# First norm taken tile by tile, weight splits of the first products put behind the rows, and transposes of the identity without a reader on TensorE

## The chip, the core and the metric

The program runs on one core of one Trainium2 chip. Its engines work side by side, each through a list of instructions of its own: TensorE (PE; its weight loads are shown as PEld), VectorE (DVE), ScalarE (ACT) and GpSimd (POOL). SyncE (SP) issues nearly all the transfers. The metric is the time of one execution on the device in microseconds (us); the median of three runs is compared.

## The reference

One layer over 512 rows of 1024 float32 numbers, and 256 memory rows. What bears on the change is its beginning:

```python
h = rmsnorm(x, g_mix_pre[l])          # x * rsqrt(mean(x*x) + EPS) * g
proj = h @ w_in[l]
aq, ak, av, iq, ik, iw, bq, bk, bv, cq, gate_logits = jnp.split(proj, split_points, axis=-1)
...
mkv = rmsnorm(mem, g_mem[l]) @ w_mem_kv[l]
...
x = x + rmsnorm(merged @ w_out[l], g_mix_post[l])
h = rmsnorm(x, g_ffn_pre[l])
gu = h @ w_ffn_in[l]
f = (jax.nn.silu(gu[..., :D_FF]) * gu[..., D_FF:]) @ w_ffn_out[l]
x = x + rmsnorm(f, g_ffn_post[l])
```

Between the projections and `merged` stand three kinds of attention: sparse attention over keys that an index (iq, ik, iw) selects, stick-breaking attention, and attention into the memory rows (with the queries cq).

## The kernel before

Every matrix product is made from split operands: a float32 number is taken as a high part of reduced precision and a low part (the rest), and a product is the sum of three passes, high by high, high by low and low by high (`passes`, L85 to L87). Making the two parts is called a split: ScalarE casts the high part (L74, or L78 with a gain), VectorE or GpSimd subtracts it from the source for the low part (L75, L79).

The stage of the change is `first` (L362 to L440). The rows x come in four tiles of 128 rows. For each tile `squares` sums the squares of its two halves (L231 on ScalarE, L229 on VectorE), `rstd1` adds them up on VectorE (L240) and raises them to the power -1/2 on GpSimd (L241), `rstd2` refines that with two small VectorE operations (L246, L247), and `scaled` multiplies the tile (L251; tiles 0 and 1 on VectorE, 2 and 3 on GpSimd). Then PE transposes each tile in eight pieces of 128 x 128 (L385). A bank of PSUM takes the piece k of two tiles, a pair, and the split of that bank with the gain of the norm (L78, L79) gives 256 columns of the transposed activations `hT[k]`. Products with two weight tiles follow, for each pair 24 passes per weight: the index keys (`w_ik`, 72 columns wide) and the first tile of cq (`w_cq`, 128 wide). The eight banks of PSUM are shared, so the transposes of the last pieces of tiles 2 and 3 wait for banks that a split of the same pair frees.

After this stage PE transposes a table (L331), makes another (L341), and goes on with four index-query tiles (`feat_tiles` with the columns from C_IQ), of which each needs a load of 512 KB by SyncE (L95, three buffers `wraw`), a cast (L74) and a low part (L75). The memory rows are loaded and normed beside these.

What sets the order: PE's list is in the order in which the code is written, in the whole program. In `first` VectorE, ScalarE and GpSimd are in written order too. Outside it a scheduler of the framework orders them; so in the kernel before, the splits of the first two index-query tiles stand on VectorE and ScalarE between the splits of pair 0 and those of pair 1. Each engine works its list strictly in order, as does SyncE with its transfers.

Of the kernel before, what the change touches and what calls it, by code (L numbers as in the profile page):

```python
# [17 lines left out]
P = 128  # L18
T = 512
D = 1024  # L20
NK = D // P
# [11 lines left out]
C_AQ, C_AK, C_AV, C_IQ, C_IK, C_BQ, C_BK, C_BV, C_CQ, C_G = (  # L33
    0, 512, 1024, 1536, 2048, 2120, 2632, 3144, 3656, 4168)
# [13 lines left out]
class Layer:  # L48
# [32 lines left out]
    def passes(self, out, pairs, first, last, **kw):  # L81

        n = len(pairs)
        for i, (sh, sl, mh, ml) in enumerate(pairs):
            self.nc.tensor.matmul(out, lhsT=sh, rhs=mh, start=first and i == 0, stop=False, **kw)  # L85
            self.nc.tensor.matmul(out, lhsT=sh, rhs=ml, start=False, stop=False, **kw)  # L86
            self.nc.tensor.matmul(out, lhsT=sl, rhs=mh, start=False, stop=last and i == n - 1, **kw)  # L87
# [90 lines left out]
        self.nc.tensor.matmul(out, lhsT=x, rhs=y[:, 0:n], start=True, stop=False)  # L178
        self.nc.tensor.matmul(out, lhsT=x, rhs=y[:, T:T + n], start=False, stop=True)  # L179

    def feat_tiles(self, w_src, acts, out, js, n=T, t0=0, evac=None):

        per = T // n
        for j in js:
            w = self.weights(w_src[:, j * P:(j + 1) * P], NK, P)
            ps = self.bank()
            yield from self.feat(ps[:, 0:n], w, acts, n=n, t0=t0)
            if evac is not None:
                out[j] = evac(ps)
                continue  # L190
            if j % per == 0:
                slot = self.big("act")
            o = (j % per) * 2 * n
            out[j] = slot[:, o:o + n], slot[:, o + n:o + 2 * n]
            self.split(*out[j], ps[:, 0:n])
# [65 lines left out]
    def run(self):  # L261
        w_in, w_kv = self.a["w_in"], self.a["w_mem_kv"]
        late = ExitStack()
        att = ExitStack()
        self.att = att.enter_context(self.tc.tile_pool(name="att", bufs=1))
        with self.tc.manual_schedule(engines={mybir.EngineType.PE}):
            self.setup()
            memT, mk, mv, cq = [], {}, {}, {}
            self.index_keys(cq)
            xs = [self.load_rows(self.a["mem"], t) for t in range(2)]  # L270
            for x in xs:
                self.norm_in(x)

            self.iq = {}
            iqs = lambda js: self.feat_tiles(w_in[:, C_IQ:C_IQ + 512], self.hT, self.iq, js, T - P, P,
                                             lambda ps: self.evac_q(ps[:, 0:T - P], T - P))
            cqs = lambda js: self.feat_tiles(w_in[:, C_CQ:C_CQ + 512], self.hT, cq, js)
            mks = lambda js: self.feat_tiles(w_kv[:, 0:512], memT, mk, js, n=M)
            mvs = self.tok_tiles(w_kv[:, 512:1024], memT, (0, 1), mv)
            memTs = self.mem_T(xs, memT)  # L280
            iq = self.add(iqs(range(4)))
            kv = self.add(cqs((1,)), self.mix(memTs, cqs((2,)), 2), mks(range(4)), cqs((3,)), mvs)
            self.drain(iq)
            self.scores()
            self.drain(kv)
            a, aq = self.qkv(C_AQ, C_AK, C_AV)
            self.branch_c(cq, mk, mv)
            self.acc = {}
            self.add(self.merge(2, self.outC, "w_up_c"))
            self.drain(aq)  # L290
            self.select()
            self.fill(FM)
            b, bq = self.qkv(C_BQ, C_BK, C_BV)
            self.branch_a(*a)
            self.drain(bq)
            self.add(self.merge(0, self.outA, "w_up_a"))
            self.outB = []
            self.add(self.merge(1, self.outB, "w_up_b"))
            self.branch_b(*b)
            self.drain()  # L300
            att.close()
            self.late = late.enter_context(self.tc.tile_pool(name="late", bufs=1))
            self.mix_out()
            self.ffn()
        late.close()
# [56 lines left out]
    def first(self, x, row, w_ik, w_cq):  # L362

        nc = self.nc
        self.hT = [self.pair("h") for _ in range(NK)]
        self.first_ps = self.bank(), self.bank()
        half = [slice(0, 256), slice(256, 512)]
        ms, bank = {}, {}

        def squares(t):  # L370
            ms[t] = self.squares([x[t][:, 0:512], x[t][:, 512:1024]], both=True)

        def mean(t):
            ms[t] = self.rstd1(ms[t])

        def scale(t):
            self.scaled(x[t], x[t], self.rstd2(ms[t]), nc.gpsimd if t > 1 else None)

        def trans(t, ks=range(NK)):
            for k in ks:  # L380
                b = t // 2, k
                if b not in bank:
                    bank[b] = self.bank()
                c = (t % 2) * P
                nc.tensor.transpose(bank[b][:, c:c + P], x[t][:, k * P:(k + 1) * P], self.ident)  # L385

        def split(pr, k):
            hi, lo = self.hT[k]
            self.split_gain(hi[:, half[pr]], lo[:, half[pr]], bank[pr, k][:, 0:256], self.cols[:, k:k + 1])

        def product(pr, i, k, w):
            c = (72, P)[i]
            self.feat_k(self.first_ps[i][0:c, half[pr]], w, self.hT, k, n=256, t0=256 * pr, c=c)

        squares(0)
        mean(0)
        ps = self.bank()
        nc.tensor.transpose(ps[:, 0:8], row, self.ident[0:8, 0:8])
        nc.vector.tensor_copy(self.cols[:, 0:8], ps[:, 0:8])
        squares(1)  # L400
        mean(1)
        scale(0)
        trans(0, range(5))
        scale(1)
        trans(1, range(5))
        trans(0, range(5, NK))
        trans(1, range(5, NK))
        ik = self.parts(w_ik, ("act", "act"), nc.gpsimd)
        squares(2)
        mean(2)  # L410
        split(0, 0)
        squares(3)
        split(0, 1)
        mean(3)
        scale(2)
        split(0, 2)
        split(0, 3)
        scale(3)
        split(0, 4)
        split(0, 5)  # L420
        cq = self.parts(w_cq, ("act", "act"), nc.gpsimd)
        split(0, 6)
        split(0, 7)
        for k in range(NK):
            product(0, 0, k, ik)
            if k > 3:
                trans(2, (k - 4,))
        for k in range(4):
            trans(3, (k,))
            split(1, k)  # L430
        for k in range(4, NK):
            trans(2, (k,))
            trans(3, (k,))
            split(1, k)
            product(0, 1, k - 4, cq)
        for k in range(4, NK):
            product(0, 1, k, cq)
        for i, w in enumerate((ik, cq)):
            for k in range(NK):
                product(1, i, k, w)  # L440
# [120 lines left out]
    def heads(self, prob, v, out, gap, first):  # L561


        p, pT = {}, {}
        for s in range(9):
            if s < 8:
                p[s] = []
            if s:
                pT[s - 1] = []
            for i in range(NT):  # L570
                if s < 8:
                    p[s].append(prob(s, i))
                if s and i < 3:
                    self.values_T(p[s - 1], i, pT[s - 1])
                if s and i == 3:
                    self.values(pT[s - 1], v, s - 1, out)
                self.fill(gap)
            if s == 0:
                self.fill(first)
# [341 lines left out]
    def ffn(self):  # L921
# [17 lines left out]
        for j, w in enumerate(self.first_ffn):  # L939
            u = (self.bank(), self.bank()), w  # L940
            run(products(*u, 0))
            first.append(u)
# [9 lines left out]
        for j, u in enumerate(first[1:], 1):  # L952
            run(products(*u, 1))
            self.gated(u[0], out(j))
# [9 lines left out]
        class Parts:  # L964
            def __getitem__(_, k):
# [3 lines left out]
                return pairs[k]  # L969

        run(self.tok_pair(w_out, Parts(), NF, range(NT), tail=4))


# [16 lines left out]
```

## Time and profile before

| | us |
|---|---|
| median of 3 runs | 917.26 (917.25 to 917.41) |
| the profiled execution | 917.32 |
| its span, first to last instruction | 915.5 |
| PE busy in the span | 887.9 (97%) |
| VectorE busy | 644.4 (70%) |
| ScalarE busy | 457.6 (50%) |
| GpSimd busy | 122.3 (13%) |

Times in the rows count from the start of the span. A row of a timeline names its start, its length, the engine, the line, the operation, what is written and read, and in brackets how long the engine had been idle before it and what ended that. Rows of one kind that follow each other are taken together (x4), and their length is then that of the whole group. PE's instructions overlap: the distance of two starts says more than the length of one.

### The profile page before, as it was taken

What the parts mean: (1) busy time and instruction counts of PE and PEld (TensorE: products, weight loads), DVE (VectorE), ACT (ScalarE), POOL (GpSimd) and SP (SyncE); (2) the same over time, 40 slices, a digit from 0 to 9 for tenths busy, and PEclk for the clock granted to TensorE, in tenths of its full rate; (3) what the DMA queues carried; (4) which work ended last, traced back from release to release, by engine and by line L of the source; (5) the groups of instructions that cost most, each with busy time, mean ns of one, the idle gap of its engine ahead of it and who ended that gap; (6) DMA issues with size and microseconds to landing.
All of it is one profiled execution on the core that took longest, in us unless ns stands there. A gap on an engine that the chain in (4) does not pass through costs nothing.

```text
span 915.5 us, 13446 instructions
## 1 busy us (share of the span) xinstructions
PE 887.9 (97%) x5110; PEld 780.3 (85%) x5110; DVE 644.4 (70%) x1122; ACT 457.6 (50%) x804; POOL 122.3 (13%) x155
## 2 busy tenths in 40 slices
PE   5999999999999999999999999899999999999997
PEld 4889788888888888888788788899999999888885
DVE  7579999963588976777563478688888887932215
ACT  6365575332576666665353355355555555821111
POOL 4000000020032304443212123400000000000000
PEclk9999999999999999999999999899999999999999
DMA  6433543444354433222473524203334334533102
GB/s 213 127 93 116 175 125 93 127 119 112 103 150 127 127 82 92 69 59 58 136 252 107 184 83 125 69 28 112 107 102 116 97 112 131 168 93 100 38 0 92
DMA packets 129541, 101.17 MB, mean 111 GB/s; under 512 B 4652, under 2 KB 115292, under 8 KB 129476
## 3 DMA queue, kind: packets, MB, share of 16 engines
q1 hardware_dynamic: 128884, 99.26, 37.2%
q10 hardware_dynamic: 592, 1.05, 0.3%
q8 instruction: 40, 0.66, 0.3%
q14 instruction: 25, 0.20, 0.1%
HBM read 93.73 MB, written 2.12 MB: 105 GB/s over the span
## 4 chain that ended last, share of the span: by engine, by line
PE 82%; DVE 9%; issue 3%; ACT 2%; DMA 1%; POOL 1%; POOLq 0%; DVEq 0%; SPq 0%; ACTq 0%
PE bank L85 19%; PE bank L86 19%; PE bank L87 19%; PE bank L734 15%; DVE wl L75 3%; PE bank L534 2%; PE bank L549 1%; PE bank L179 1%; PE bank L178 1%; PE bank L209 1%; PE bank L211 1%; PE bank L210 1%; DMA lraw<-in_w_ffn_in_dram 1%; DVE e L621 1%; DVE score L506 1%
## 5 line engine op out<-in xcount | busy, mean ns | idle before, releaser
L75 DVE TENSOR_TENSOR wl<-wraw,wh 128x1024 fp32r<-128x1024 f32 (+1 forms) x112 | 130.6, 1167 | 100.4 <-ACT wh L74 100.1
L74 ACT CAST wh<-wraw 128x1024 fp32r<-128x1024 f32 (+1 forms) x112 | 107.3, 959 | 141.7 <-PE bank L86 79.5
L85 PE MATMUL bank<-h,wh 128*128 128x512 f32 (+1 forms) x376 | 148.8, 396 | 0.0
L87 PE MATMUL bank<-h,wl 128*128 128x512 f32 (+1 forms) x376 | 145.3, 386 | 1.0 <-DVE wl L75 0.9
L86 PE MATMUL bank<-h,wh 128*128 128x512 f32 (+1 forms) x376 | 145.0, 386 | 0.0
L734 PE MATMUL bank<-w,act 128*128 128x512 f32 x360 | 89.0, 393 | 0.0
L87 PEld LDWEIGHTS bank<-h,wl 128*128 128x128 f32 x376 | 70.6, 188 | 15.9 <-DVE wl L75 1.7
L85 PEld LDWEIGHTS bank<-h,wh 128*128 128x128 f32 x376 | 70.9, 189 | 11.7 <-PE bank L341 0.2
L86 PEld LDWEIGHTS bank<-h,wh 128*128 128x128 f32 x376 | 70.8, 188 | 11.4
L734 PEld LDWEIGHTS bank<-w,act 128*128 128x128 f32 x360 | 67.4, 188 | 15.0
L734 PE MATMUL bank<-wh,act 128*128 128x512 f32 x240 | 72.5, 393 | 0.0
L85 PE MATMUL bank<-act,wh 128*128 128x256 f32 (+1 forms) x204 | 69.2, 339 | 0.7 <-DVE s L896 0.7
L86 PE MATMUL bank<-act,wh 128*128 128x256 f32 (+1 forms) x204 | 67.9, 333 | 0.0
L87 PE MATMUL bank<-act,w 128*128 128x256 f32 x228 | 64.1, 281 | 0.0
L85 PE MATMUL bank<-h,w 128*128 128x256 f32 x228 | 64.1, 281 | 0.0
L86 PE MATMUL bank<-h,w 128*128 128x256 f32 x228 | 64.1, 281 | 0.0
L87 PE MATMUL bank<-h,w 128*128 128x256 f32 x228 | 64.1, 281 | 0.0
L85 PE MATMUL bank<-act,w 128*128 128x256 f32 x228 | 64.1, 281 | 0.0
L86 PE MATMUL bank<-act,w 128*128 128x256 f32 x228 | 64.1, 281 | 0.0
L241 POOL TENSOR_TENSOR rs<-ms,mhalf 128x1 f32<-128x1 f32 x18 | 12.1, 674 | 387.7 <-DVE ms L240 384.0
L598 POOL TENSOR_TENSOR p<-toep,score 128x128 f32<-128x128 f32 (+3 forms) x32 | 31.6, 1001 | 199.2 <-DVE score L507 103.0
L734 PEld LDWEIGHTS bank<-wh,act 128*128 128x128 f32 x240 | 45.0, 188 | 9.9
(189 smaller groups left out, 2113.3 us busy)
## 6 DMA issues: line engine op xcount, KB each, us to landing
wraw<-in_w_in_dram SPq DMA_DIRECT2D x64, 512.0 KB, 3.6
lraw<-in_w_ffn_in_dram SPq DMA_DIRECT2D x22, 512.0 KB, 3.9
wraw<-in_w_ffn_in_dram SPq DMA_DIRECT2D x22, 512.0 KB, 3.7
wraw<-in_w_ffn_out_dram SPq DMA_DIRECT2D x11, 512.0 KB, 3.6
lraw<-in_w_ffn_out_dram SPq DMA_DIRECT2D x11, 512.0 KB, 3.5
wraw<-in_w_mem_kv_dram SPq DMA_DIRECT2D x8, 512.0 KB, 3.7
lraw<-in_w_out_dram SPq DMA_DIRECT2D x6, 512.0 KB, 5.5
wraw<-in_w_out_dram SPq DMA_DIRECT2D x6, 512.0 KB, 3.7
```

Of the source, the lines that this page charges most:

```text
L74: self.nc.scalar.copy(hi, src)
L75: (eng or self.nc.vector).tensor_tensor(lo, src, hi.bitcast(F32), op=OP.subtract)
L85: self.nc.tensor.matmul(out, lhsT=sh, rhs=mh, start=first and i == 0, stop=False, **kw)
L86: self.nc.tensor.matmul(out, lhsT=sh, rhs=ml, start=False, stop=False, **kw)
L87: self.nc.tensor.matmul(out, lhsT=sl, rhs=mh, start=False, stop=last and i == n - 1, **kw)
L178: self.nc.tensor.matmul(out, lhsT=x, rhs=y[:, 0:n], start=True, stop=False)
L179: self.nc.tensor.matmul(out, lhsT=x, rhs=y[:, T:T + n], start=False, stop=True)
L209: self.nc.tensor.matmul(ps, lhsT=ah[:, s], rhs=wh[:, k2], start=st, stop=False)
L241: self.nc.gpsimd.tensor_tensor(r, ms, self.mhalf, op=OP.pow)
L534: self.nc.tensor.transpose(ps[:, c:c + P], p[i][:, j * P:(j + 1) * P], self.ident)
L598: nc.gpsimd.tensor_tensor(s, toep[0][:, 0:n][:, ::-1], self.mask[i], op=OP.add)
L734: self.nc.tensor.matmul(ps[c], lhsT=st_[:, s], rhs=mv_[:, 0, c * 512:(c + 1) * 512], start=f and k == order[0], stop=l and k == order[-1])
```

## The change

`squares` in `first` now takes for each tile whether VectorE shares in it: tiles 0 and 3 are halved between ScalarE and VectorE as before, tiles 1 and 2 are squared by ScalarE alone. Tile 0 is scaled and its first four pieces are transposed before tile 1 is summed on VectorE. The pieces are transposed 4 and 4, before 5 and 3. The low parts of `w_ik` and `w_cq` are made by VectorE, before by GpSimd; that of `w_cq` and its cast stand behind all eight splits of pair 0. The first two index-query tiles are loaded in `first`, and split behind the splits of pair 1; `feat_tiles` takes these two from a list. `warm(n)` writes n transposes of the identity into a bank that nothing reads: 5 and 21 around the transpose of the gain, and 10 between the first pieces of tile 0 and those of tile 1.

```diff
--- before.py
+++ after.py
@@ -178,11 +178,11 @@
         self.nc.tensor.matmul(out, lhsT=x, rhs=y[:, 0:n], start=True, stop=False)
         self.nc.tensor.matmul(out, lhsT=x, rhs=y[:, T:T + n], start=False, stop=True)
 
-    def feat_tiles(self, w_src, acts, out, js, n=T, t0=0, evac=None):
+    def feat_tiles(self, w_src, acts, out, js, n=T, t0=0, evac=None, ws=()):
 
         per = T // n
         for j in js:
-            w = self.weights(w_src[:, j * P:(j + 1) * P], NK, P)
+            w = ws[j] if j < len(ws) else self.weights(w_src[:, j * P:(j + 1) * P], NK, P)
             ps = self.bank()
             yield from self.feat(ps[:, 0:n], w, acts, n=n, t0=t0)
             if evac is not None:
@@ -273,7 +273,7 @@
 
             self.iq = {}
             iqs = lambda js: self.feat_tiles(w_in[:, C_IQ:C_IQ + 512], self.hT, self.iq, js, T - P, P,
-                                             lambda ps: self.evac_q(ps[:, 0:T - P], T - P))
+                                             lambda ps: self.evac_q(ps[:, 0:T - P], T - P), self.w_iq)
             cqs = lambda js: self.feat_tiles(w_in[:, C_CQ:C_CQ + 512], self.hT, cq, js)
             mks = lambda js: self.feat_tiles(w_kv[:, 0:512], memT, mk, js, n=M)
             mvs = self.tok_tiles(w_kv[:, 512:1024], memT, (0, 1), mv)
@@ -367,8 +367,8 @@
         half = [slice(0, 256), slice(256, 512)]
         ms, bank = {}, {}
 
-        def squares(t):
-            ms[t] = self.squares([x[t][:, 0:512], x[t][:, 512:1024]], both=True)
+        def squares(t, both):
+            ms[t] = self.squares([x[t][:, 0:512], x[t][:, 512:1024]], both=both)
 
         def mean(t):
             ms[t] = self.rstd1(ms[t])
@@ -392,24 +392,34 @@
             c = (72, P)[i]
             self.feat_k(self.first_ps[i][0:c, half[pr]], w, self.hT, k, n=256, t0=256 * pr, c=c)
 
-        squares(0)
+
+        idle = self.bank()
+
+        def warm(n):
+            for _ in range(n):
+                nc.tensor.transpose(idle[:, 0:P], self.ident, self.ident)
+
+        squares(0, True)
         mean(0)
+        warm(5)
         ps = self.bank()
         nc.tensor.transpose(ps[:, 0:8], row, self.ident[0:8, 0:8])
         nc.vector.tensor_copy(self.cols[:, 0:8], ps[:, 0:8])
-        squares(1)
+        warm(21)
+        scale(0)
+        trans(0, range(4))
+        squares(1, False)
         mean(1)
-        scale(0)
-        trans(0, range(5))
         scale(1)
-        trans(1, range(5))
-        trans(0, range(5, NK))
-        trans(1, range(5, NK))
-        ik = self.parts(w_ik, ("act", "act"), nc.gpsimd)
-        squares(2)
+        warm(10)
+        trans(1, range(4))
+        trans(0, range(4, NK))
+        trans(1, range(4, NK))
+        ik = self.parts(w_ik, ("act", "act"))
+        squares(2, False)
         mean(2)
         split(0, 0)
-        squares(3)
+        squares(3, True)
         split(0, 1)
         mean(3)
         scale(2)
@@ -417,10 +427,10 @@
         split(0, 3)
         scale(3)
         split(0, 4)
-        split(0, 5)
-        cq = self.parts(w_cq, ("act", "act"), nc.gpsimd)
-        split(0, 6)
-        split(0, 7)
+        w_iq = [self.load(self.a["w_in"][:, C_IQ + j * P:C_IQ + (j + 1) * P], NK, P) for j in range(2)]
+        for k in (5, 6, 7):
+            split(0, k)
+        cq = self.parts(w_cq, ("act", "act"))
         for k in range(NK):
             product(0, 0, k, ik)
             if k > 3:
@@ -435,6 +445,7 @@
             product(0, 1, k - 4, cq)
         for k in range(4, NK):
             product(0, 1, k, cq)
+        self.w_iq = [self.parts(w) for w in w_iq]
         for i, w in enumerate((ik, cq)):
             for k in range(NK):
                 product(1, i, k, w)
```

VectorE, from the start of the program to the first split of pair 0 (`ss`, `ms`, `rs` and `rt` are the sums and factors of the norm, `act` with 1024 columns a tile of x, `cols` the gain, `act<-wraw,act` the low part of `w_ik`). Before:

```order
L229 ISA junk,ss<-act 128x512
L229 ISA ss 128x1
L240 TENSOR_SCALAR ms<-ss 128x1
L246 SCALAR_TENSOR_TENSOR rt<-rs,ms 128x1
L247 SCALAR_TENSOR_TENSOR rs<-rt,rs 128x1
L251 TENSOR_SCALAR act<-act,rs 128x1024
L246 SCALAR_TENSOR_TENSOR rt<-rs,ms 128x1
L247 SCALAR_TENSOR_TENSOR rs<-rt,rs 128x1
L251 TENSOR_SCALAR act<-act,rs 128x1024
```

These begin with the squares of tile 1, behind those of tile 0 and the copy of the gain. Now the same place reads:

```order
L246 SCALAR_TENSOR_TENSOR rt<-rs,ms 128x1
L247 SCALAR_TENSOR_TENSOR rs<-rt,rs 128x1
L251 TENSOR_SCALAR act<-act,rs 128x1024
L240 TENSOR_SCALAR ms<-ss 128x1
L246 SCALAR_TENSOR_TENSOR rt<-rs,ms 128x1
L247 SCALAR_TENSOR_TENSOR rs<-rt,rs 128x1
L251 TENSOR_SCALAR act<-act,rs 128x1024
L75 TENSOR_TENSOR act<-wraw,act 128x576
```

The squares of tile 1 are gone from VectorE, its sum stands behind the scaling of tile 0, and the low part of `w_ik` behind the scaling of tile 1.

VectorE, from the last four splits of pair 0 to the splits of pair 1 and of the index-query weights (`h` is hT, `wl` the low part of an index-query tile, `act<-wraw,act` with 1024 columns that of `w_cq`), as a difference:

```order
 L247 SCALAR_TENSOR_TENSOR rs<-rt,rs 128x1
 L79 SCALAR_TENSOR_TENSOR h<-bank,cols,h 128x256 x4
+L75 TENSOR_TENSOR act<-wraw,act 128x1024
+L79 SCALAR_TENSOR_TENSOR h<-bank,cols,h 128x256 x8
 L75 TENSOR_TENSOR wl<-wraw,wh 128x1024 x2
-L79 SCALAR_TENSOR_TENSOR h<-bank,cols,h 128x256 x8
```

The eight splits of pair 1 stood behind the two index-query low parts; now they stand ahead of them, and behind the one of `w_cq`.

PE, from the start of the program to the first products (`ident` is the identity, `rows_75` the gain of the norm, `act` a tile of x), as a difference:

```order
-L398 MATMUL bank<-ident,rows_75 128x8
-L385 MATMUL bank<-ident,act 128x128 x16
+L400 MATMUL bank<-ident 128x128 x5
+L406 MATMUL bank<-ident,rows_75 128x8
+L400 MATMUL bank<-ident 128x128 x21
+L385 MATMUL bank<-ident,act 128x128 x4
+L400 MATMUL bank<-ident 128x128 x10
+L385 MATMUL bank<-ident,act 128x128 x12
 L85 MATMUL bank<-h,act 72x256
```

The ten stand between the four pieces of tile 0 and all that PE does with tile 1; what follows the sixteen transposes is as before. From the table of L331 on, the order of every engine is the same in both kernels.

## Rows read from the trace of the kernel before

**Rows 1.** The page, its first part: busy time, share of the span and instructions of each engine.

```profile
PE 887.9 (97%) x5110; PEld 780.3 (85%) x5110; DVE 644.4 (70%) x1122; ACT 457.6 (50%) x804; POOL 122.3 (13%) x155
```

**Rows 2.** PE's waits in the whole program, by what was waited for: us in total, times, the longest.

```profile
PE bank L385 <- DVE act L251: 5.7, 2, 4.6
PE bank L359 <- DVE h L79: 4.4, 2, 2.9
PE bank L398 <- DMA rows<-in_g_mix_pre_dram: 3.1, 1, 3.1
...
PE bank L385 <- DVE h L79: 1.7, 1, 1.7
```

**Rows 3.** VectorE's timeline in the first 48 us.

```profile
5.75 0.69 DVE L229 CUSTOM_DVE_ANT_0 junk<-act 128x512 f32<-128x512 f32 x1 [0.17 <-DMA act<-in_x_dram]
...
6.71 0.21 DVE L246 SCALAR_TENSOR_TENSOR rt<-rs,ms 128x1 f32<-128x1 f32 x1
...
7.15 0.75 DVE L251 TENSOR_SCALAR act<-act,rs 128x1024 f32<-128x1024 f32 x1
7.97 1.37 DVE L246 SCALAR_TENSOR_TENSOR rt<-rs,ms 128x1 f32<-128x1 f32 x1
...
9.57 0.75 DVE L251 TENSOR_SCALAR act<-act,rs 128x1024 f32<-128x1024 f32 x1
...
11.40 0.48 DVE L79 SCALAR_TENSOR_TENSOR h<-bank,cols,h 128x256 fp32r<-128x256 f32 x1
...
14.04 0.72 DVE L246 SCALAR_TENSOR_TENSOR rt<-rs,ms 128x1 f32<-128x1 f32 x1
...
14.87 1.65 DVE L79 SCALAR_TENSOR_TENSOR h<-bank,cols,h 128x256 fp32r<-128x256 f32 x4
16.44 4.36 DVE L75 TENSOR_TENSOR wl<-wraw,wh 128x1024 fp32r<-128x1024 f32 x2
20.72 3.21 DVE L79 SCALAR_TENSOR_TENSOR h<-bank,cols,h 128x256 fp32r<-128x256 f32 x8
29.95 0.20 DVE L332 COPY cols<-bank 128x40 f32<-128x40 f32 x1 [6.02 <-PE bank L331]
...
36.41 1.23 DVE L75 TENSOR_TENSOR wl<-wraw,wh 128x1024 fp32r<-128x1024 f32 x1 [2.59 <-ACT wh L74]
```

**Rows 4.** GpSimd's timeline in the same stretch.

```profile
5.67 0.55 POOL L241 TENSOR_TENSOR rs<-ms,mhalf 128x1 f32<-128x1 f32 x1 [3.65 <-DVE cols L399]
...
7.91 1.41 POOL L75 TENSOR_TENSOR act<-wraw,act 128x576 fp32r<-128x576 f32 x1
...
13.63 1.12 POOL L251 TENSOR_SCALAR act<-act,rs 128x1024 f32<-128x1024 f32 x1
...
16.20 2.38 POOL L75 TENSOR_TENSOR act<-wraw,act 128x1024 fp32r<-128x1024 f32 x1
```

**Rows 5.** ScalarE's timeline in the same stretch.

```profile
5.82 0.63 ACT L231 ACTIVATE junk<-act 128x512 f32<-128x512 f32 x1 [0.61 <-DMA act<-in_x_dram]
...
30.25 0.63 ACT L231 ACTIVATE junk<-act 128x512 f32<-128x512 f32 x1
...
35.33 1.05 ACT L74 CAST wh<-wraw 128x1024 fp32r<-128x1024 f32 x1 [4.36 <-PE bank L86]
```

**Rows 6.** PE's timeline in the same stretch.

```profile
10.38 2.61 PE L385 MATMUL bank<-ident,act 128*128 128x128 f32 x11 [1.10 <-DVE act L251]
12.64 0.56 PE L85 MATMUL bank<-h,act 128*72 128x256 f32 x1
...
15.77 0.28 PE L87 MATMUL bank<-h,act 128*72 128x256 f32 x1
...
17.29 0.93 PE L385 MATMUL bank<-ident,act 128*128 128x128 f32 x7
...
21.25 0.44 PE L385 MATMUL bank<-ident,act 128*128 128x128 f32 x2 [1.66 <-DVE h L79]
...
29.66 0.25 PE L331 MATMUL bank<-ident,rows 40*128 40x40 f32 x1
```

**Rows 7.** Busy time by stretch: the stretch and its length, then the busy time of PE, PEld, DVE, ACT and POOL with the number of instructions, the granted clock of PE, the share of the transfer engines and GB/s.

```profile
21.25:29.66 8.41, 8.41 (x70) 8.28 (x71) 2.68 (x7) 1.53 (x3) 0.00 (x0) 1.00 0.69 208
31.08:43.98 12.90, 12.90 (x75) 12.74 (x74) 9.16 (x19) 6.08 (x13) 1.53 (x3) 1.00 0.42 124
```

**Rows 8.** The clock: the same table for three stretches (the first products, and two in the middle of the program), and PE's timeline there.

```profile
12.64:15.56 2.92, 2.92 (x15) 2.90 (x14) 2.85 (x10) 2.92 (x8) 2.12 (x3) 1.00 0.41 130
...
575.00:576.00 1.00, 0.00 (x0) 0.00 (x0) 1.00 (x3) 0.00 (x0) 0.00 (x0) 0.77 0.00 0
...
577.00:578.00 1.00, 1.00 (x6) 1.00 (x6) 0.12 (x1) 0.48 (x1) 1.00 (x1) 0.50 0.68 185
...
582.00:583.00 1.00, 1.00 (x9) 1.00 (x7) 0.00 (x0) 0.41 (x1) 1.00 (x1) 0.81 0.00 0
...
576.79 0.69 PE L359 MATMUL bank<-ident,act 128*128 128x128 f32 x2 [2.86 <-DVE h L79]
...
577.49 0.41 PE L86 MATMUL bank<-h,act 128*128 128x256 f32 x1
577.70 0.41 PE L87 MATMUL bank<-h,act 128*128 128x256 f32 x1
```

**Rows 9.** SyncE's queue in the first 30 us: the issue of the first memory rows' transfer; the length is that of the issuing.

```profile
21.24 2.24 SPq L348 DMA_DIRECT2D act<-in_mem_dram  x1
```

## Prediction

> **What bounds the kernel now.** I read the page first: TensorE (PE) is busy for 97% of the span [rows 1], so a change can only give what PE loses. Then PE's waits: outside the middle and the end of the program they are the input, the first norm and its splits [rows 2]. Then the order of time on each engine over the first 48 us, and the clock.
>
> The stage that the change touches runs from 0 to 29.66 us, where PE takes up the transpose of L331 [rows 6]. From there PE has hardly a gap (12.90 us busy of 12.90 from 31.08) [rows 7], so the moment at which it leaves this stage sets the end. The last wait in the stage decides that moment: PE stands until 21.25 for VectorE's low part h L79 [rows 6], and after that nothing holds it: 8.41 us of back to back work up to 29.66. So the question is when the transposes that now start at 21.25 can start.
>
> They need a bank that is freed by the first L79 of rows 256 to 511. On VectorE that one starts at 20.72, behind the two index-query splits (4.36 us from 16.44) [rows 3]. The first of these ran beside GpSimd's split of the same shape (16.20, 2.38 us) [rows 4]; alone such a split takes 1.23 us [rows 3], so some 2 us of the 4.36 are the two engines getting in each other's way. The same shows twice before: a 128x1 L246 takes 1.37 us instead of 0.21 beside GpSimd's split at 7.91, and 0.72 us beside its scaling at 13.63 [rows 3, 4].
>
> The clock: the column for the granted clock reads 1.00 here, but the first products come at 0.21 us each (15 instructions in 2.92 us, one of them the tail of a transpose) [rows 8], the same as the 0.21 from 577.49 to 577.70, where the column reads 0.50 [rows 8]; later they come at 0.12 (70 in 8.41 us) [rows 7]. The quicker step sets in at about 15.8: the pass at 15.77 is the first of 0.28 us where such a pass at the low clock has 0.41 [rows 6, 8]. I go by the steps: 1.2 GHz until about 15.8 us, 2.4 GHz from there. Before the rise PE had worked without a gap from 10.38.
>
> **The change part by part.** Times are those of the profiled execution: span 915.5 us, 917.32 with what lies around it (1.8 us), 0.06 above the median of 917.26.
>
> *Norm of tile 0.* VectorE no longer squares half of tile 1 (0.69 us plus its read) [rows 3] ahead of the L246 of tile 0. GpSimd's power ends at 5.67 + 0.55 = 6.22; L246, L247 and L251 follow as the rows have them (0.44 from the start of L246 to that of L251, then 0.75) [rows 3, 4], and end at 7.45 instead of 7.90. Gain 0.45.
>
> *Norm of tile 1.* Both halves of its squares now lie on ScalarE: 5.82 + 2 x 0.7 (0.63 and the read of the sum) = 7.2 [rows 5]. VectorE's sum follows the scaling of tile 0 (7.45 to 7.65), the power ends at about 8.3, and L246 is not held, since GpSimd no longer splits: L251 runs 8.75 to 9.5 instead of 9.57 to 10.32. Gain 0.8, to PE at 9.55.
>
> *The index-key split moves to VectorE*, behind that L251: 128x576 on VectorE is not in the trace; it lies between the 0.48 of 256 columns (L79) and the 1.23 of 1024 [rows 3], and by its width at 0.75, to 10.25. The first bank reaches ScalarE at about 10.1 and VectorE at 10.65, so the split is covered; without that cover it would cost its 0.75.
>
> *Splits of rows 0 to 255.* The first L79 comes at 10.65 instead of 11.40. The middle of this chain stays as it is, with tile 3's L246 still behind GpSimd's scaling (1.12 us), all of it 0.7 earlier: the last four L79 end at 15.8 instead of 16.5.
>
> *The query split* (w_cq) goes from GpSimd to VectorE, behind these eight: 1.2 us, to 17.0. Its ScalarE half (1.05 us for such a cast, now after all eight of pair 0) ends at about 14.9 and is in time [rows 5]. *The two index-query splits* leave this place, taking 4.36 us with them. So the first L79 of rows 256 to 511 starts at 17.0 (its cast needs PE's products of rows 0 to 255, done at about 16.2, then transposes and 0.47 us: 16.95, level with it). That is 3.7 before 20.72. PE takes up its transposes at about 17.6 instead of 21.25, with one query product left between: **3.65 us earlier**.
>
> *After that* VectorE needs 3.2 us for eight L79, to 20.2, while PE comes to them from 20.2 on at 0.36 each. The index-query splits follow, 20.3 to 22.7; PE needs the first at 31.08 - 3.65 = 27.4. Cover 6 us; VectorE was idle for 6.02 us there, to 29.95 [rows 3]. What is late next is the queue of SyncE: the load of the second index-query tile now waits for VectorE's index-key split (10.25, before: GpSimd's, 9.32) and holds the small tables behind it, not read before 26; the fourth load and the memory rows go from 21.24 to about 23 [rows 9]. ScalarE squares those rows at 30.25 (26.6 now), then stands 4.36 us for PE [rows 5]: a wait of 1 to 2 us there is hidden. I cost these edits at nothing.
>
> *Unread transposes*, 5, 21 and 10 of the identity. Their operation isn't shown on the identity alone; the nearest rows are the kernel's own transposes: eleven from 10.38 to 12.64, 0.21 each at the low clock, seven in 0.93 us, 0.13 each, at the high one [rows 6]. From the identity's writing (about 1.7) the first 26 end at 7.75 at the low clock: 0.25 behind tile 0, whose transposes wait for nothing else. If the clock rises among them, the ten end before tile 1 is there or up to 0.4 behind it; I took that into the 10.1 above. If it doesn't, they cost: the first rival. Ends: nothing, and the 3 us of that rival.
>
> The rest of the program keeps its order on every engine, so 3.65 is carried whole: 917.3 - 3.65 = **913.6**, with 0.3 either way from the sum.
>
> **A second place for the clock.** In the middle PE stands 2.86 us until 576.79; during that wait the granted clock falls to 0.50, at about 575.5 by the 0.77 of that microsecond, and rises at about 582.4 by the 0.81 of its [rows 8]. PE works 5.6 us at half speed: 2.8 us lost. Nothing in the change is near it, but everything arrives 3.65 us earlier, and the profile doesn't show that the fall keeps its place against the wait. Bounds: no fall, 2.8 us gained; a rise 3.1 us after the first product (12.64 to 15.8), as at the start: 1.2 us gained; or the same, which I take, since it is this place's own row.
>
> **The rivals.**
> *The unread transposes don't raise the clock.* For it: of the time before 15.8 only the last 3.1 us (from 12.64) were products, and a rise after products alone fits as well. Against: PE was already transposing from 10.38 [rows 6]. Then the ten sit in front of tile 1: 7.75 + 4 x 0.21 + 10 x 0.21 = 10.7 instead of 9.55, products begin at 13.2, and the rise comes 3.1 us (as at the start) to 5.6 us later (as at 576.79). With 24 products at 0.21 until then, the transposes start at 19.05 to 20.4: gain 2.2 to 0.85, **915.1 to 916.5**. The Trainium skill, "TensorE: Matmul & The Clock Gate", Part 4, states just this: transposes don't count as work for the clock the way matmuls do. By that rule the time would be this rival's; no run here shows a stretch of transposes alone.
>
> *Shorter half-speed stretch in the middle*: 1.2 us on top of the sum, **912.4**.
>
> *Slower*: as the first rival, but the clock stays low for one more such stretch as between its fall and rise (575.5 to 582.4, 6.8 us). Place: the 96 products of this stage, each 0.09 dearer. 6.8 us at 0.21 instead of 0.12 lose 3.0: the 0.85 becomes minus 2.1, **919.4**. It decides from the point where the rise is later than about 20.7 us. Against it: the clock rose within 5.6 us of steady products both times.
>
> *No carry*: a load or a memory row holds the index queries and gives it back, **917**. Against it: the slack of 6 and 4 us above.
>
> **How the numbers follow.** A kernel here can be told from no change at about 0.2%, 1.83 us. Forecast 0.59 (913.6, its own range 913.2 to 914.1), shorter stretch 0.20, cold transposes 0.14, no carry 0.04, slower 0.03. Faster: 0.79 and the quarter of the cold case that gains over 1.83 us, 0.83; slower: its own 0.03 and a part of no carry, 0.04; same: the rest, 0.13. The range goes from 911.9 (shorter stretch, with the sum's 0.3 and a little) to 915.4, which takes in the first fifth of the cold case; what lies above it (0.11 of the cold case, no carry, slower) is some 0.18.
>
> **What would show it.** Right: L251 of tile 1 ends near 9.5; every 128x1 L246 of tiles 0 and 1 takes 0.21; no VectorE split of weights above 1.3 us; first products 0.12 apart; no PE gap over 1 us between 13 and 26; L331 near 26.0. Wrong: first products 0.21 apart, L331 past 27.5, a PE wait for a weight split after 27, or L331 early and the end not.

## The result, and the profile after

| us | before | after |
|---|---|---|
| median of four runs | 917.25 (915.79 to 917.41) | 911.43 (910.88 to 912.45) |
| the profiled execution | 917.32 | 910.88 |
| its span | 915.5 | 909.1 |
| start of the transpose of L331 (end of the changed stage) | 29.66 | 26.16 |

The ratio of the times is 0.9941, with an interval of 0.9924 to 0.9959: faster. The predicted 913.6 is 2.2 us too high, and the time lies 0.5 us below the range. The stage gave 3.5 us of the 5.8, close to the 3.65 of the sum; the other 2.3 came from elsewhere, in the two profiled executions mainly from the clock in the middle of the program, where the change edits nothing.

The page's first part and PE's waits in the whole program, which answer to [rows 1, 2]:

```profile
PE 888.3 (98%) x5146; PEld 780.1 (86%) x5146; DVE 641.5 (71%) x1120; ACT 458.6 (50%) x808; POOL 117.1 (13%) x153
```

```profile
PE bank L359 <- DVE h L79: 4.4, 2, 2.9
...
PE bank L385 <- DVE act L251: 1.4, 2, 1.1
PE bank L86 <- DVE h L79: 1.1, 3, 0.6
```

The 5.7 us behind the first scaling [rows 2] are 1.4, partly because the unread transposes now stand in that time, and the 1.7 us of L385 behind L79 are gone. In their place are three short waits of the first products. The 4.4 us of L359, in the middle of the program, are as they were.

VectorE in the first stage, which answers to [rows 3]:

```profile
6.74 0.75 DVE L251 TENSOR_SCALAR act<-act,rs 128x1024 f32<-128x1024 f32 x1
...
8.29 0.22 DVE L246 SCALAR_TENSOR_TENSOR rt<-rs,ms 128x1 f32<-128x1 f32 x1 [0.67 <-POOL rs L241]
...
8.74 0.75 DVE L251 TENSOR_SCALAR act<-act,rs 128x1024 f32<-128x1024 f32 x1
9.41 0.75 DVE L75 TENSOR_TENSOR act<-wraw,act 128x576 fp32r<-128x576 f32 x1
...
13.05 0.71 DVE L246 SCALAR_TENSOR_TENSOR rt<-rs,ms 128x1 f32<-128x1 f32 x1
...
13.88 1.65 DVE L79 SCALAR_TENSOR_TENSOR h<-bank,cols,h 128x256 fp32r<-128x256 f32 x4
15.45 1.21 DVE L75 TENSOR_TENSOR act<-wraw,act 128x1024 fp32r<-128x1024 f32 x1
17.02 3.23 DVE L79 SCALAR_TENSOR_TENSOR h<-bank,cols,h 128x256 fp32r<-128x256 f32 x8 [0.36 <-ACT h L78]
20.51 2.36 DVE L75 TENSOR_TENSOR wl<-wraw,wh 128x1024 fp32r<-128x1024 f32 x2 [0.26 <-ACT wh L74]
26.45 0.20 DVE L332 COPY cols<-bank 128x40 f32<-128x40 f32 x1 [3.58 <-PE bank L331]
```

The L246 of tile 1 takes 0.22 us where it took 1.37 beside GpSimd's split, and the two index-query splits take 2.36 us for both where they took 4.36. The eight splits of pair 1 start at 17.02, held at the end by ScalarE's cast and no longer by VectorE's own list. GpSimd still scales tile 2 beside the L246 at 13.05, which still takes 0.71.

PE in the same stretch, which answers to [rows 6]:

```profile
1.66 1.33 PE L400 MATMUL bank<-ident 128*128 128x128 f32 x5 [1.66 <-POOL mhalf L324]
...
3.12 3.31 PE L400 MATMUL bank<-ident 128*128 128x128 f32 x21
7.55 0.66 PE L385 MATMUL bank<-ident,act 128*128 128x128 f32 x4 [1.12 <-DVE act L251]
8.04 1.25 PE L400 MATMUL bank<-ident 128*128 128x128 f32 x10
...
14.41 0.34 PE L86 MATMUL bank<-h,act 128*72 128x256 f32 x1 [0.65 <-DVE h L79]
...
26.16 0.25 PE L331 MATMUL bank<-ident,rows 40*128 40x40 f32 x1
```

and a table by stretch, with the columns of [rows 7], for two pieces among the unread transposes and for the end of the stage:

```profile
3.00:4.00 1.00, 1.00 (x5) 0.98 (x6) 0.00 (x0) 0.00 (x0) 0.00 (x0) 1.00 0.92 360
5.00:6.00 1.00, 1.00 (x12) 1.00 (x10) 0.51 (x4) 0.41 (x3) 0.29 (x1) 1.00 1.15 299
...
17.21:26.16 8.95, 8.95 (x78) 8.82 (x76) 5.40 (x10) 4.79 (x10) 0.00 (x0) 1.00 0.59 152
```

Some five instructions a microsecond from 3 to 4, some twelve from 5 to 6: the unread transposes get quicker at about 4.7 us, and until then PE had done nothing but transposes, since 1.66. The granted clock's column reads 1.00 in both rows, so the steps have to be read here, as at the start of the kernel before. From 17.21 to 26.16 PE is busy without a gap.

The middle of the program, the same place as in [rows 8]: PE's wait, and the clock behind it.

```profile
572.80 0.44 PE L359 MATMUL bank<-ident,act 128*128 128x128 f32 x2 [2.86 <-DVE h L79]
```

```profile
573.00:574.00 1.00, 1.00 (x11) 1.00 (x9) 0.35 (x2) 0.47 (x1) 1.00 (x1) 1.00 0.66 189
577.00:578.00 1.00, 1.00 (x11) 1.00 (x11) 0.55 (x2) 0.53 (x2) 1.00 (x2) 1.00 0.00 0
```

The wait is the same 2.86 us, but behind it PE does eleven instructions a microsecond at a granted clock of 1.00, where it did six at 0.50 [rows 8]. This is what made the time lower than forecast. Of the 917.32 - 910.88 = 6.44 us between the two profiled executions, 3.50 are there at L331; at the end of this wait it is 576.79 - 572.80 = 3.99 us, and what is left, some 2.5, is this stretch. The 0.49 between the two places was not traced to a cause; from L331 to the end of this wait the profiles of all versions that were not filled there take from 546.5 to 547.1 us, those of the two kernels overlapping.

### The profile page after: what moved, and what is told of

It is laid out like the page before. It is cut to its first block, busy times and chain, and to the rows that moved or that the text cites. A ratio compares the mean times of both kernels' runs of the same rounds, so it can differ in the third digit from the quotient of the medians.

```text
span 909.1 us, 13518 instructions
## 1 busy us (share of the span) xinstructions
PE 888.3 (98%) x5146; PEld 780.1 (86%) x5146; DVE 641.5 (71%) x1120; ACT 458.6 (50%) x808; POOL 117.1 (13%) x153
## 4 chain that ended last, share of the span: by engine, by line
PE 82%; DVE 10%; issue 3%; ACT 2%; POOL 2%; DMA 1%; POOLq 0%; DVEq 0%; ACTq 0%
PE bank L85 19%; PE bank L86 19%; PE bank L87 19%; PE bank L745 15%; DVE wl L75 3%; PE bank L545 2%; PE bank L560 1%; PE bank L179 1%; PE bank L178 1%; PE bank L209 1%; PE bank L211 1%; PE bank L210 1%; DMA lraw<-in_w_ffn_in_dram 1%; DVE e L632 1%; POOL rs L241 1%
## 5 line engine op out<-in xcount | busy, mean ns | idle before, releaser
L75 DVE TENSOR_TENSOR wl<-wraw,wh 128x1024 fp32r<-128x1024 f32 (+1 forms) x112 | 128.5, 1149 | 101.3 <-ACT wh L74 101.0
L87 PEld LDWEIGHTS bank<-h,wl 128*128 128x128 f32 x376 | 70.6, 188 | 15.8 <-DVE wl L75 1.7
```

What stands on the lines that cost most here:

```text
L75: (eng or self.nc.vector).tensor_tensor(lo, src, hi.bitcast(F32), op=OP.subtract)
```

## The experiments

Two questions were open: whether the missing half-speed stretch in the middle belongs to the change or only to the execution that was seen, and which part of the change gives the 3.5 us of the first stage. For the second the start of L331 is the measure, since the times carry the first.

**The changed kernel once more.** No edit.

> The changed kernel once more, for its spread. Theory A (3.5 us come from the first stage; the rest is the half-speed stretch in the middle, whose place against PE's wait there changes from run to run): L331 at 26.2 us in the profile; the times lie between 910.8 (nothing lost in the middle) and 913.7 (2.8 us lost, as in the profile of before), and the mean granted clock goes with them: 0.998 near 911, 0.995 to 0.996 from 911.8 on. Of the kernel before, some runs lie below 917.2, too. Theory B (the whole 5.8 us are the change's own work, some of it late in the program): every run within 0.3 us of 911.4, whatever its clock.

Measured: 912.36 (912.22 to 913.38), ratio 0.9959 (0.9947 to 0.9972). The profiled execution is the one of 913.38, span 911.6, L331 at 26.20. In the middle it has:

```profile
572.79 0.69 PE L359 MATMUL bank<-ident,act 128*128 128x128 f32 x2 [2.85 <-DVE h L79]
```

```profile
573.00:574.00 1.00, 1.00 (x6) 1.00 (x6) 0.13 (x1) 0.47 (x1) 1.00 (x1) 0.50 0.77 206
577.00:578.00 1.00, 1.00 (x7) 1.00 (x7) 0.48 (x1) 0.41 (x1) 0.00 (x0) 0.50 0.08 16
```

The same program, the same wait to 0.01 us, and this time the clock falls: six instructions a microsecond at 0.50. The spans differ by 2.5 us. So the fall isn't set by the program alone: it differs from execution to execution, which is called a draw below.

**The wait in the middle filled.** Twenty transposes of the identity, whose result nobody reads, behind the second pair of the middle's transposes, where PE stands, in both kernels:

```diff
+            if k == 2:
+                for _ in range(20):
+                    nc.tensor.transpose(first[2][0][0][:, 256:384], self.ident, self.ident)
```

> The changed kernel with 20 unread transposes of the identity in the middle, where PE stands 2.86 us for a bank (between the second and the third pair of transposes of L359); 2.6 us of work by the 0.13 each that they take. Theory A: PE no longer stands, the clock cannot fall, so every run has a mean clock of 0.998 and a time of 910.9 within 0.3 us, and the profile shows 1.00 in each microsecond from 565 to 585. Theory B: the same spread as the changed kernel, 910.9 to 912.5.

> The kernel before with the same 20 unread transposes in the middle, its start untouched. Theory A: 2.8 us faster than the usual run of before, 914.5 within 0.3 us, clock 0.998 in all runs, L331 at 29.7 as before. Theory B: 917.3, since the start is not touched.

Measured on the changed kernel: 910.67 (910.35 to 910.75), ratio 0.9938 (0.9926 to 0.9951). PE's timeline there:

```profile
569.62 2.35 PE L958 MATMUL bank<-ident 128*128 128x128 f32 x20
572.64 0.44 PE L359 MATMUL bank<-ident,act 128*128 128x128 f32 x2 [0.67 <-DVE h L79]
```

The real work after the wait starts no later than it did (572.64, before 572.80), the clock stays at 1.00, and the spread of five runs is 0.4 us where the changed kernel alone had 1.2 and 1.6 us in its two sets. This is the best version of all that ran.

Measured on the kernel before: 915.59 (914.14 to 915.79), ratio 0.9986 (0.9977 to 0.9995), in two groups: five runs at 914.1 to 914.5, six at 915.6 to 915.8. The profiled one, 914.49, has 1.00 throughout the middle. The upper group wasn't explained, so this kernel ran again below.

**The changed kernel without the 36 unread transposes of the start** (`warm(5)`, `warm(21)` and `warm(10)` taken out).

> The changed kernel without its 36 unread transposes at the start. If they raise the clock (A): products at 0.21 us each for the first 3 us or so, but VectorE's splits set the pace there, so L331 at 26.2 to 27.0 us, at most 0.8 later than with them. If they do nothing (C): the first products are at the same step with and without them, L331 at 26.2 or, without the time that they take, earlier. Time: the changed kernel's plus what L331 moves, with the same spread of up to 2.8 us from the middle.

Measured: 912.43 (911.29 to 913.21), ratio 0.9958 (0.9945 to 0.9972), L331 at 26.33. The products step at 0.21 until about 13.4 us, and still L331 is only 0.17 later than with them: with them, the first products wait for VectorE's splits. In the middle this profile has a third outcome, a fall of about half the length:

```profile
572.86 0.44 PE L359 MATMUL bank<-ident,act 128*128 128x128 f32 x2 [2.86 <-DVE h L79]
```

```profile
574.00:576.00 2.00, 2.00 (x11) 2.00 (x11) 0.81 (x2) 0.47 (x1) 1.39 (x2) 0.50 1.13 340
576.00:578.00 2.00, 2.00 (x17) 2.00 (x16) 0.48 (x1) 0.80 (x2) 0.22 (x1) 0.84 0.31 93
```

The granted clock is back on its way up between 576 and 578 (0.84 on the mean), where the whole fall of after_again still has 0.50. From the end of the wait to the end of its span of 910.6 us it takes 337.8 us; the changed kernel without a fall took 336.3, with the whole one 338.8. So a whole fall costs 2.5 us and the shorter one 1.5. The profiles of before_iq and after_pool, both below, have the shorter fall too.

**One part alone.** The index-query tiles loaded early and split behind pair 1, and nothing else of the change, in the kernel before:

```diff
+        w_iq = [self.load(self.a["w_in"][:, C_IQ + j * P:C_IQ + (j + 1) * P], NK, P) for j in range(2)]
...
+        self.w_iq = [self.parts(w) for w in w_iq]
```

> The kernel before with one part of the change alone: the first two index-query tiles are loaded in the first stage and split behind the splits of rows 256 to 511. By the prediction's rows: VectorE is free for these splits from 16.5, their casts need PE's transposes (17.7, done at 18.2), GpSimd's query split now runs alone and ends by 18.6: PE takes up its transposes at 18.8 instead of 21.25, L331 at 27.2 us, 2.4 of the 3.5 us. Rival (the contention of the two engines is what costs, not the order): L331 at 28 or later.

Measured: 913.74 (912.44 to 914.0), ratio 0.9963 (0.9947 to 0.9979), L331 at 27.73: 1.93 of the 3.50 us. PE takes up its transposes at 18.79, as expected (18.8), but then needs 8.94 us to L331 and not the 8.41 of the kernel before, so that 27.2 was missed by half a microsecond.

**One part undone.** The low parts of `w_ik` and `w_cq` back on GpSimd, in the changed kernel:

```diff
-        ik = self.parts(w_ik, ("act", "act"))
+        ik = self.parts(w_ik, ("act", "act"), nc.gpsimd)
...
-        cq = self.parts(w_cq, ("act", "act"))
+        cq = self.parts(w_cq, ("act", "act"), nc.gpsimd)
```

> The changed kernel with the low parts of the index-key and the query weights back on GpSimd. If the two engines block each other: L246 of tile 1 takes 1.3 to 1.4 us again, L251 of tile 1 ends near 10.9 instead of 9.5, L331 at 27.4 us (1.2 later). Rival (the splits on GpSimd are hidden): L246 0.22 us, L331 at 26.2 or earlier, since VectorE has 2 us less to do.

Measured: 914.49 (914.28 to 914.58), ratio 0.9978 (0.9967 to 0.999), L331 at 27.92, 1.76 later than in the changed kernel. VectorE, GpSimd and PE there:

```profile
8.25 1.37 DVE L246 SCALAR_TENSOR_TENSOR rt<-rs,ms 128x1 f32<-128x1 f32 x1 [0.67 <-POOL rs L241]
...
9.85 0.75 DVE L251 TENSOR_SCALAR act<-act,rs 128x1024 f32<-128x1024 f32 x1
...
18.15 3.40 DVE L79 SCALAR_TENSOR_TENSOR h<-bank,cols,h 128x256 fp32r<-128x256 f32 x8 [1.50 <-ACT h L78]
```

```profile
8.18 1.42 POOL L75 TENSOR_TENSOR act<-wraw,act 128x576 fp32r<-128x576 f32 x1
```

```profile
18.75 0.39 PE L87 MATMUL bank<-h,act 128*128 128x256 f32 x1 [0.37 <-POOL act L75]
```

The L246 beside GpSimd's split is back at 1.37 us. By these rows it stands until the split ends: it ends at 9.62 and the split at 9.60, as in the kernel before (7.97 + 1.37 = 9.34, the split 7.91 + 1.41 = 9.32 [rows 3, 4]). Tile 1 is scaled 1.1 us later by it (9.85, before 8.74), and the splits of pair 1 start 1.1 later. The rest of the 1.76, some 0.6, comes behind the low part of `w_cq` on GpSimd, for which PE stands until 18.75; the expectation, with L331 at 27.4, didn't have it.

**The order of the norm undone.** Tile 1 squared by both engines ahead of the scaling of tile 0, in the changed kernel:

```diff
+        squares(1, True)
+        mean(1)
         scale(0)
         trans(0, range(4))
-        squares(1, False)
-        mean(1)
```

> The changed kernel with the squares of tile 1 halved again and in front of the scaling of tile 0, as before; all else as changed. By the rows: L251 of tile 0 ends at 7.9 instead of 7.5, but L246 of tile 1 is no longer held by a split on GpSimd, so L251 of tile 1 ends at 9.2, no later than now; the ten unread transposes then end at about 9.75, so the norm tile by tile buys nothing by itself: L331 at 26.0 to 26.4. Rival (the norm tile by tile gives the 0.8 us that the prediction gave to it): L331 at 27.0.

Measured: 913.46 (912.35 to 913.83), ratio 0.9958 (0.9944 to 0.9973), L331 at 26.20, 0.04 later. The order of the norm gives nothing that the end of the stage shows. It brings tile 0 forward (its scaling starts at 7.22 here, 6.74 with the new order) but sets tile 1 back (8.49 here, 8.74 with it), and here the ten unread transposes hold tile 1's transposes until 9.61. The profile has the low stretch in the middle (granted clock about 0.50 from 572 to 578).

**The unread transposes of the start alone**, in the kernel before (`warm` at the same three places).

> The kernel before with the 5, 21 and 10 unread transposes alone. If they raise the clock (A): the first products come at 0.12 instead of 0.21 us each, but PE then waits for VectorE, and L331 stays at 29.3 to 29.7 us. If they do nothing (C): first products at 0.21, and the ten delay the transposes of tile 1, L331 at 29.7 or later. Time: 917.3 less at most 0.4, and up to 2.8 less in a run where the clock does not fall in the middle.

Measured: 915.69 (915.25 to 917.35), ratio 0.9994 (0.9983 to 1.0004), L331 at 29.36: 0.3 earlier. With the 0.17 above, they give 0.2 to 0.3 us at L331 (0.1 between the two filled versions of the changed kernel below, 26.11 and 26.23).

**The upper group of the filled kernel before.** The same kernel two more times, then with the unread transposes of the start as well, and the changed kernel filled in the middle but without those of the start:

> The same kernel as before_fill, run again, since its executions fell into two groups (914.1 to 914.5 and 915.6 to 915.8) and the one profile was of the lower. Theory A (the middle can be lost in one more way, with a shorter low stretch even when filled): a profile of the upper group has L331 at 29.7 and some 1.4 us more between 560 and 600. Theory B (the start draws, since in the kernel before the clock rises only among the first products): a profile of the upper group has L331 at 31.1 and the rest of the program as in the lower. Theory C (another wait of PE elsewhere, such as the input's or the end's): both as in the lower group, and a low granted clock in some third place. The two groups again in its times, 914.3 and 915.7.

> Once more the same kernel, for one further profile: either 914.3 or 915.7, with what theory A (low stretch at the filled place), B (L331 late by 1.4) or C (a third place) expects of the upper group.

> The kernel before with the 36 unread transposes of the start and the 20 of the middle. Theory B: with both places covered one group is left, at 914.3 less 0.35 (L331 29.36 as in before_warm), 913.7 to 914.2, no spread above 0.5. Theories A and C: two groups 1.4 apart, 913.9 and 915.3.

> The changed kernel with the fill of the middle and without the 36 transposes of the start. Theory B: two groups, 910.8 (L331 26.3) and one 1 to 1.5 above it, and this is what the dummies of the start buy. Theories A and C: after_fill showed one group with the dummies, and so this one has one group as well, at 910.8 (0.15 above after_fill).

Measured: before_fill_again 914.46 (914.31 to 915.88), ratio 0.9983 (0.9974 to 0.9992), again in two groups, six runs at 914.3 to 914.5 and five at 915.3 to 915.9; before_fill_third 914.52; before_fill_warm 914.5 (914.24 to 915.97), ratio 0.9984 (0.9975 to 0.9993), with three of eleven runs at 915.8 to 916.0; after_fill_nowarm 911.38 (910.9 to 911.73), ratio 0.9945 (0.9932 to 0.9959), no second group. The other eight runs of before_fill_warm, 914.2 to 914.8, are no faster than the lower group without the transposes of the start.

Two of these profiles fell into the upper group, before_fill_again with 915.77 and before_fill_warm with 915.78, and their L331 starts at 31.03 and 30.88, where before_fill_third has 29.73. From there on both are as in the lower group. The place is theory B's, but its reason isn't: the clock had risen long before, at about 15 us and, in before_fill_warm, ahead of all products, and it falls again behind a wait. PE's timeline and the table by stretch of before_fill_again:

```profile
21.09 0.44 PE L385 MATMUL bank<-ident,act 128*128 128x128 f32 x2 [1.64 <-DVE h L79]
...
22.61 0.41 PE L87 MATMUL bank<-h,act 128*128 128x256 f32 x1
22.82 0.41 PE L85 MATMUL bank<-h,act 128*128 128x256 f32 x1
...
31.03 0.26 PE L331 MATMUL bank<-ident,rows 40*128 40x40 f32 x1
```

```profile
22.00:23.00 1.00, 1.00 (x6) 1.00 (x5) 1.00 (x4) 0.51 (x2) 0.00 (x0) 0.50 1.07 287
24.00:25.00 1.00, 1.00 (x7) 1.00 (x7) 0.00 (x0) 0.00 (x0) 0.00 (x0) 0.50 1.23 385
```

and L331 in before_fill_third:

```profile
29.73 0.25 PE L331 MATMUL bank<-ident,rows 40*128 40x40 f32 x1
```

PE stands until 21.09 for the same split as in the kernel before [rows 6], and behind that wait the passes are 0.21 apart at a granted clock of 0.50 until about 25: 31.03 - 29.73 = 1.3 us. So the kernel before has, its last 5 us apart, two waits behind which the clock may fall, the 1.66 us before 21.25 and the 2.86 us in the middle, and the change takes the first away. In none of the profiles of the changed kernel or of its versions, after_pool's among them, is L331 late by such a fall; their longest wait between 13 and 26 us is 0.66.

## Why the prediction was right and wrong

**What bounds the kernel, and the sum of the stage: right.** The moment at which PE leaves the stage sets the end, apart from the clock: the lower group of the filled kernel before takes 914.1 to 914.5, the filled changed kernel 910.35 to 910.75, some 3.6 us for a gain of 3.50 at L331 (29.66 to 26.16). By its steps: tile 0 scaled at 7.49 (forecast 7.45), tile 1 at 9.49 (8.75 to 9.5), the index-key split 0.75 (0.75), the first L79 at 10.42 (10.65), the last four ended at 15.53 (15.8), the query split 1.21 (1.2), the first L79 of pair 1 at 17.02 (17.0). PE takes up its transposes at 17.21, 0.4 sooner than forecast. But here a term of the sum was too small: from there it has 78 instructions and 8.95 us up to L331, not the 8.41 of the kernel before, since it arrives with more left to do. The two make 26.16 against 26.0. Of the 3.65 us, 3.50 came.

**What gives it.** The index-query splits behind pair 1 give 1.93 alone, and GpSimd's two low parts on VectorE 1.76 when they are undone; that is 3.7 for 3.5, so the two nearly add up. The gain on tile 1 came as forecast, but from the index-key split's move off GpSimd and not from the norm taken tile by tile: with the split back on GpSimd tile 1's scaling is 1.1 us later and takes the splits of pair 1 along (after_pool), with the old order of the norm it is 0.25 earlier (after_norm). The gain on tile 0 is worth nothing here by itself. And the end of the chain has moved: VectorE is done with its list at 16.66 and stands 0.36 us for ScalarE's cast.

**The edits costed at nothing: right.** The index-query splits end at 22.87 (forecast 22.7) and PE doesn't wait for them. The memory rows' transfer goes to 23.32 (about 23), their squares to 29.64, 3.0 later than the 26.6 forecast, where 1 to 2 us were allowed for; ScalarE still stands 1.46 us for PE afterwards, so no cost came of it.

**The unread transposes: the first rival is wrong.** The clock rises at about 4.7 us, with transposes alone behind it, and the products step at 0.12 from the first. The Trainium skill, "TensorE: Matmul & The Clock Gate", Part 4, says that a transpose doesn't count as work for the clock in the way a matmul does. The rows of the changed kernel differ, and so does after_fill: with twenty transposes in the wait the clock held. For float32 transposes of 128 x 128 the measurement decides. Where it rises is a draw too: in after_fill, with the same start, seven instructions lie in the microsecond from 6 to 7 and twelve in that from 8 to 9.

**The step that failed: "A second place for the clock".** It named the 2.8 us of the middle, gave "no fall, 2.8 us gained" as a bound, and then took "the same", because it was this place's own row; and the cases and the range held only the shorter stretch (912.4). The step took one execution's row for a property of the kernel. The runs show a draw: the changed kernel has 910.88 with no fall and 913.38 with a whole one, behind waits of 2.86 and 2.85 us, so that a whole fall costs 2.5 us and not 2.8. Five of its nine runs lie between, at 912.2 to 912.5, which is the time of the rival with the shorter stretch and of after_nowarm's profile (912.43), which shows one. With a whole fall the sum stood: 917.3 - 3.65 = 913.65, and 913.38 was measured. That the first four runs gave 911.43 was the luck of the draw: the median of all nine is 912.35.

**The number to start from.** The median of 917.26 came from three runs, all of the dearer group of this kernel. Over 58 runs that stood beside the others the kernel before lies at 914.35 to 917.99, two of them below 915, where the lower group of the filled kernel lies, 28 at 915.4 to 916.2 and 28 above 916.8; the mean is 916.5. The nine runs of the changed kernel have a mean of 912.1. So the gain that can be expected is some 4.4 us, not 5.8. An estimate from the filled kernels gives 4.2 of it: 3.6 from the stage, and 0.6 from the fall behind the wait at 21.25, which has lost its wait; it cost 1.3 us, by the two groups in 11 of the 23 runs of the filled kernel before. The first four runs of each kernel made 5.8 of the 4.4: before with 917.25, 0.75 above its mean, after with 911.43, 0.67 below its. That the clock could fall behind the stage's own wait was not in the prediction at all.

**What stays open.** What decides in an execution whether the clock falls behind a wait wasn't found; the length of the wait doesn't tell (2.86 us without a fall, 2.85 and 2.86 with one). The Trainium skill, same page, Part 1, states for the start of a kernel that the same kernel has different numbers of slow matmuls in different runs, because the chip looks at PE's activity on a beat that the start of the kernel doesn't set. The two rises at the start (after at about 4.7 us, after_fill at about 7) agree with it, the two executions of the changed kernel differ in the same way behind a wait in the middle, and no run here tests its reason. What makes the 916 group of the unfilled kernel before wasn't seen in a profile either: only one of its executions was profiled, and above the 914.3 of the filled one's lower group the fall of the stage (1.3 us) and the shorter one of the middle (1.3 to 1.5 us in the three profiles that have it) give nearly the same time. And after_fill_nowarm was 0.7 us above after_fill, of which L331 explains 0.12 in the profiles; the two ran on different chips.

## What to carry to other kernels

Look for every wait of TensorE long enough that the clock has been seen to fall behind one (here 1.64 and 2.86 us), and price it twice, with the fall and without: it can be a draw of some tenths of a per cent that an edit far away seems to win or lose. Where the wait can't be removed, unread transposes in it cost nothing that the rows show and took the draw away, which here was worth 1.7 us (912.36 to 910.67) beside the 3.5 of the stage; at the start of the program unread transposes bought 0.1 to 0.3 us at L331 and nothing clear in times from one chip, since the products waited for other things. On VectorE and GpSimd, elementwise work of the same moment is not always parallel work: a 128x1 L246 stood until GpSimd's split or scaling ended, while four splits L79, which read PSUM, kept their 0.41 us each beside GpSimd's scaling of tile 3 (the splits from 13.88 to 15.53, the scaling 1.12 us from 14.12). Two splits given to GpSimd cost 1.76 us here.

## What the runs showed that was not expected

The fall of the clock is not repeated from execution to execution: 2.86 us of waiting and no fall, 2.86 us and a fall that cost 1.5 us, 2.85 us and one that cost 2.5, 1.64 us and one that cost 1.3. With twenty unread transposes in the wait of the middle the granted clock stayed at 1.00 there in all six profiled executions that had them.

The column of the granted clock reads 1.00 at the start of the program while transposes start five to the microsecond, and 0.50 later for the same steps: there the steps have to be read, not the column.
